# Two decoder blocks on one core: the tokens' factors as rows, by DRAM and GpSimd's queue instead of a product with ones

## The chip, the cores and the metric

The kernel runs on one core of a Trainium2 chip. The metric is the device time of one launch in microseconds. Time before: 1255.82 us, the median of three runs (1255.24 to 1256.68).

## What is computed

The reference chains two networks on 256 tokens of 1024 features. The first has two layers (a mixer of attention and a state-space part, then a mixer with a gated linear recurrence), the second has two attention layers with a shared memory. Each layer ends with a gated feed-forward part. Every part begins with an RMS norm, and that is what matters here:

```
def _rmsnorm(x, g):
    x32 = x.astype(jnp.float32)
    y = x32 * lax.rsqrt(jnp.mean(x32 * x32, axis=-1, keepdims=True) + EPS)
    return (y * g.astype(jnp.float32)).astype(x.dtype)

def swiglu(x, w_gate, w_up, w_down):
    return (jax.nn.silu(x @ w_gate) * (x @ w_up)) @ w_down
```

The factor of a token, the rsqrt, is one number for each of the 256 tokens. It commutes with the matrix product, so the kernel multiplies with the weights first and applies the factor to the product.

## The kernel before

TensorE multiplies in pairs of a rounded and a remainder part: each 512 KB tile of weights (`wr`, loaded by SyncE's queue) is rounded by ScalarE into `wh` (line 217), and VectorE subtracts to get the remainder `wl` (line 195). Four `wr` buffers, six `wh`/`wl` pairs, fifteen slots of 128 x 512 for intermediate results (`s`), six PSUM banks for products (`pm`) and two for transposes (`pt`).

The residual at the end of a part (`residual`) runs for the first half of the tokens and then for the second. It computes a mean square and asks GpSimd for a power of -1/2 (`rsqrt`, line 414, a column of 128 partitions by 1). In the first network that happens twice per half: once for the norm after the part, on which VectorE waits before it adds to `x`, and once for the factor `r` of the part that follows. In the second network only the latter exists.

With tokens in partitions, `r` is a column and can be used as a scale of one instruction. Where a product has features in partitions (`wide_t`, `linear_t`), the tokens lie along the free dimension, and the factors are wanted as a row of 256 numbers, the same in all partitions. `spread_rows` makes that: VectorE multiplies the identity by `r` for each half (`d`, line 208), TensorE multiplies a matrix of ones by `d` in plain fp32 (line 220, `pt<-s,ones`), and ScalarE copies the result to a slot (line 217, `s<-pt`). It is called five times: in each of the four `ffn` calls, after the first 512 hidden features, and once in `odd_mixer`, the recurrent mixer.

The order of the work is written by the program and by a running count of TensorE's time: `later(delay, fn)` puts a piece of work off until `pe_time` has advanced by that many microseconds, `poll` issues what is due, and `need(key)` issues what a reader must have now. `spread_rows` puts its product off by `TUNE["rows"]`, 2.0. The recording layer then sets the order within each engine.

The first reader in `ffn` is the multiply of `s` by `both` on VectorE, after a whole `wide_t` of 256 hidden features; the first in `odd_mixer` is the multiply of a bank by `rows` into `xb`, after a `linear_t` of 512 features.

Of the kernel before, what the change touches and what calls it, by code (L numbers as in the profile page):

```python
# [9 lines left out]
F32 = mybir.dt.float32  # L10
# [3 lines left out]
ALU = mybir.AluOpType  # L14
AX = mybir.AxisListType
PSUM = bass.MemoryType.PSUM

P = 128
D = 1024
# [22 lines left out]
TUNE = {  # L42
    "mla_share": 0,
    "mla_share2": 0.25,
    "lru_share": 0.35,
    "mj0": 4.5,
    "mj1": 4.5,
    "mh0": 0.0,
    "mh1": 4.5,
    "mi0": 5.0,  # L50
# [62 lines left out]
class Operand:  # L113


    def __init__(self, net, K):
        self.net, self.K = net, K
        self.quads = [None] * ((K + 3) // 4)
# [23 lines left out]
class Net:  # L142
    def __init__(self, ctx, tc, ins, plan):
        self.tc, self.nc, self.ins, self.plan = tc, tc.nc, ins, plan
        self.n = 0
        self.wall_at = 0
        self.pe_time = 0.0
        self.pending = []
        self.running = False
        self.open = []  # L150
        self.mem_r = []
        self.share = self.relief = 0.0
        e = ctx.enter_context
        self.const = e(tc.tile_pool(name="const", bufs=1))
        self.wraw = e(tc.tile_pool(name="wraw", bufs=4))
        self.wsp = e(tc.tile_pool(name="wsp", bufs=6))
        self.bigs = e(tc.tile_pool(name="bigs", bufs=11))
        self.slots = e(tc.tile_pool(name="slots", bufs=15))
        self.junk = e(tc.tile_pool(name="junk", bufs=1))
        self.small = e(tc.tile_pool(name="small", bufs=48))  # L160
        self.s5c = e(tc.tile_pool(name="s5c", bufs=1))
        self.rtab = e(tc.tile_pool(name="rtab", bufs=1))
        self.mm = e(tc.tile_pool(name="mm", bufs=6, space=PSUM))
        self.tr = e(tc.tile_pool(name="tr", bufs=2, space=PSUM))

# [198 lines left out]

    def spread_rows(self, r):

        out, d = self.slot(), self.slot()
        for h in HALVES:
            self.ts(d[:, h * P : (h + 1) * P], self.ident, r[h], ALU.mult)

        def go():
            ps = self.tbank()
            self.mmul(ps[:, 0:256], self.ones, d[:, 0:256], True, True)
            self.act(out[:, 0:256], ps[:, 0:256])

        self.later(TUNE["rows"], go, [("rows", out.name)])
        return out[:, 0:256], ("rows", out.name)

    def linear32(self, x, mat, c0, c1, sink):

# [123 lines left out]
    def ffn(self, X, r, gate, up, g_at, u_at, down, post, gains, last=False, aside=None):  # L504
        nc = self.nc
        HT = Operand(self, FF // P)
        wg = self.weights([(gate, k * P, g_at, g_at + 512) for k in range(KD)])
        wu = self.weights([(up, k * P, u_at, u_at + 512) for k in range(KD)])
        for h in HALVES:
            G, U = self.group(X, h, wg, 512), self.group(X, h, wu, 512)  # L510
            s, t = self.slot(), self.slot()
            self.act(s, G, AF.Silu, scale=r[h])
            self.mul(t, U, s)
            self.to_features(HT, h, 0, [t[:, i * P : (i + 1) * P] for i in range(4)])
        rows, key = self.spread_rows(r)
        if aside is not None:
            aside()
        mean = [self.sm() for h in HALVES]
        for h in HALVES:
            self.ts(mean[h], r[h], math.sqrt(1.0 / D), ALU.mult)  # L520
        two = lambda a: a.rearrange("p (a q) -> p a q", a=2)
        both = rows.unsqueeze(1).to_broadcast([P, 2, 256])
        for c0 in range(512, FF, 256):
            G = self.wide_t(X, gate, g_at + c0)
            self.need(key)
            s, t = self.slot(), self.slot()
            self.wide_sum(s, G)
            self.mul(two(s), two(s), both)
            self.act(s, s, AF.Silu)
            U = self.wide_t(X, up, u_at + c0)  # L530
            self.wide_sum(t, U)
            self.mul(t, t, s)
            self.heads_out(HT, c0 // P, t)
        gp = None if post is None else self.load_post(post)
        KF = FF // P
        self.flush()
        return self.rows_out(HT, down, range(KF), 5, gp, gains, last, r, mean)
# [764 lines left out]
    def odd_mixer(self, X, R):  # L1302
# [3 lines left out]
        e = self.lru_e  # L1306
# [36 lines left out]
        def conv(c):  # L1343
            self.need(("xb", c))
            for k in range(4 * c, 4 * c + 4):
                w = [self.col("conv_w", 8 * i + k) for i in range(4)]
                self.act(xc[:, k], xb[:, k], AF.Identity, scale=w[3], bias=self.col("conv_b", k))
                for lag in (1, 2, 3):
                    self.stt(xc[:, k, lag:], xb[:, k, : 256 - lag], w[3 - lag], xc[:, k, lag:], ALU.mult, ALU.add)
                self.act(v8(XH)[:, k], xc[:, k])  # L1350
                self.sub(v8(XL)[:, k], xc[:, k], v8(XH)[:, k].bitcast(F32))

        self.linear(X, "od_w_in", 0, 512, x_sink)
        self.later(TUNE["conv"], lambda: conv(0), [("xc", 0)])
        rows, key = self.spread_rows(R)
        banks = self.linear_t(X, "od_w_in", 512, 1024)
        self.need(key)
        for i, bank in enumerate(banks):
            for j in (0, 1):
                self.mul(  # L1360
# [70 lines left out]
        for i, z in enumerate(gz):  # L1431
            o = z.rearrange("p (m r j) -> p m r j", m=4, r=4)
# [405 lines left out]
```

## Time and profile before

| | |
|---|---|
| median of three runs | 1255.82 us |
| the profiled execution, its own time | 1256.24 us |
| its span on the core | 1254.5 us |
| TensorE, matmul records | busy 1237.9 us, 99% |
| VectorE | busy 879.7 us, 70% |
| ScalarE | busy 766.0 us, 61% |
| GpSimd | busy 51.3 us, 4% |
| granted TensorE clock | 0.999 of full speed |
| SyncE's load queue | 215.68 MB, 55.1% of 16 engines |

The span is the time between the core's first and last instruction; the profiled execution's own time is 1.74 us longer than its span. A busy share is taken over the whole span, and matmuls are pipelined, so that their records overlap and a busy share of 99% says that TensorE hardly ever waits, not that it works at its peak. The page's chain of waits gives 84% of the span to TensorE.

### The profile page before, as it was taken

How to read it: one execution, taken by the hardware profiler on the slowest of the kernel's cores; microseconds unless marked ns; L12 is line 12 of the kernel's file. 1: busy time of each engine (PE TensorE's matmuls, PEld its weight loads, DVE VectorE, ACT ScalarE, POOL GpSimd, SP SyncE). 2: the span in 40 equal slices, each digit the busy share in tenths (PEclk: the TensorE clock that was granted, in tenths of full speed). 3: DMA queues.
4: the chain of work that ended last, by engine and by line, in shares of the span. 5: the costliest groups of instructions: out<-in, count | busy, mean ns of one | idle time of the engine just before them, and what ended most of it. 6: DMA issues, size and time to landing. Idle time of an engine off the chain costs nothing.

```text
span 1254.5 us, 17973 instructions
## 1 busy us (share of the span) xinstructions
PE 1237.9 (99%) x6526; PEld 1036.7 (83%) x6526; DVE 879.7 (70%) x1579; ACT 766.0 (61%) x1446; POOL 51.3 (4%) x64
## 2 busy tenths in 40 slices
PE   8999999999999999999999899999999999999998
PEld 6776888888889888888887788888888888888887
DVE  7997578775588977776467855777746865677752
ACT  6767577554488766555378845555546675655531
POOL 1000000000000000000013100000000100000000
PEclk9999999999999999999999999999999999999999
DMA  8714367666555467666545224666665532666662
GB/s 269 232 52 151 118 193 230 202 189 210 154 188 178 164 193 218 191 194 204 183 150 178 85 70 149 218 185 189 213 188 152 182 118 82 205 197 187 187 198 69
DMA packets 63065, 216.83 MB, mean 173 GB/s; under 512 B 7136, under 2 KB 7520, under 8 KB 62976
## 3 DMA queue, kind: packets, MB, share of 16 engines
q1 hardware_dynamic: 62976, 215.68, 55.1%
q8 instruction: 51, 0.84, 0.3%
q14 instruction: 38, 0.31, 0.1%
HBM read 214.61 MB, written 1.05 MB: 172 GB/s over the span
## 4 chain that ended last, share of the span: by engine, by line
PE 84%; ACT 5%; DVE 5%; DMA 3%; issue 2%; POOL 1%; SPq 0%; ACTq 0%; POOLq 0%; DVEq 0%
PE pm L220 80%; PE pt L227 3%; DVE wl L195 2%; ACT j L217 1%; ACT b L217 1%; ACT wh L217 1%; DMA wr<-in_wall_dram 1%; DVE s L195 1%; ACT s L217 1%; DVE b L212 1%; POOL m L414 1%; DMA x<-in_x_dram 1%; DMA s<-in_xT_dram 1%; DMA s<-in_memT_dram 0%; ACT L217 0%
## 5 line engine op out<-in xcount | busy, mean ns | idle before, releaser
L195 DVE TENSOR_TENSOR wl<-wr,wh 128x1024 fp32r<-128x1024 f32 (+2 forms) x389 | 467.1, 1206 | 208.4 <-ACT wh L217 207.2
L220 PE MATMUL pm<-wh,b 128*128 128x512 f32 (+2 forms) x1788 | 575.4, 395 | 4.6 <-ACT wh L217 2.9
L217 ACT ACTIVATE wh<-wr 128x1024 fp32r<-128x1024 f32 (+2 forms) x381 | 397.3, 1047 | 267.2 <-PE pm L220 141.3
L220 PE MATMUL pm<-b,wh 128*128 128x512 f32 (+1 forms) x1440 | 453.2, 372 | 0.0
L220 PEld LDWEIGHTS pm<-wh,b 128*128 128x128 f32 x1788 | 334.5, 188 | 73.8 <-ACT wh L217 5.6
L220 PE MATMUL pm<-b,wl 128*128 128x256 f32 x1296 | 359.6, 278 | 0.0
L220 PE MATMUL pm<-wl,b 128*128 128x512 f32 (+2 forms) x894 | 348.8, 391 | 0.7 <-DVE wl L195 0.7
L220 PEld LDWEIGHTS pm<-b,wh 128*128 128x128 f32 x1440 | 261.1, 188 | 50.8 <-ACT b L217 0.3
L220 PEld LDWEIGHTS pm<-b,wl 128*128 128x128 f32 x1296 | 243.8, 188 | 0.3
L220 PEld LDWEIGHTS pm<-wl,b 128*128 128x128 f32 x894 | 168.6, 189 | 34.5 <-DVE wl L195 2.5
L217 ACT ACTIVATE s<-pm 128x256 f32<-128x256 f32 (+1 forms) x152 | 58.4, 386 | 66.3 <-PE pm L220 66.2
L195 DVE TENSOR_TENSOR s<-pm,s 128x256 f32<-128x256 f32 (+1 forms) x164 | 74.0, 453 | 35.5 <-ACT s L217 20.8
L414 POOL TENSOR_TENSOR m<-m,mhalf 128x1 f32<-128x1 f32 (+3 forms) x54 | 47.1, 873 | 980.2 <-DVE m L209 767.9
L195 DVE TENSOR_TENSOR s<-s,s 128x512 f32<-128x512 f32 (+3 forms) x90 | 60.5, 672 | 2.5
L217 ACT ACTIVATE b<-pt,cpk 128x128 fp32r<-128x128 f32 (+2 forms) x138 | 48.2, 390 | 8.9 <-DVE b L212 5.5
L217 ACT ACTIVATE j<-pm,m 128x128 f32<-128x128 f32 (+1 forms) x94 | 36.7, 406 | 22.4 <-PE pm L220 19.6
L227 PE MATMUL pt<-ident,s 128*128 128x128 f32 x288 | 44.1, 276 | 3.5 <-DVE s L195 2.0
L212 DVE SCALAR_TENSOR_TENSOR b<-pt,cpk,b 128x128 fp32r<-128x128 f32 x122 | 37.9, 345 | 11.4 <-ACT b L217 10.9
L227 PEld LDWEIGHTS pt<-ident,s 128*128 128x128 f32 x288 | 34.0, 142 | 14.4 <-issue 3.3
L217 ACT ACTIVATE j<-x 128x512 f32<-128x512 f32 x32 | 20.2, 631 | 27.0 <-DVE x L212 13.9
L220 PE MATMUL pm<-s,b 128*128 128x256 f32 (+1 forms) x160 | 34.6, 337 | 0.0
L220 PE MATMUL pm<-wr,s 128*128 128x512 f32 x72 | 33.4, 602 | 0.1
(162 smaller groups left out, 809.8 us busy)
## 6 DMA issues: line engine op xcount, KB each, us to landing
wr<-in_wall_dram SPq DMA_DIRECT2D x381, 512.0 KB, 3.7
wr<-in_wall_dram SPq DMA_DIRECT2D x11, 256.0 KB, 3.6
s<-in_memT_dram SPq DMA_DIRECT2D x8, 256.0 KB, 5.8
s<-in_gpost_dram SPq DMA_DIRECT2D x8, 256.0 KB, 4.8
wr<-in_wall_dram SPq DMA_DIRECT2D x4, 384.0 KB, 3.0
x<-in_x_dram SPq DMA_DIRECT2D x2, 512.0 KB, 6.9
s<-in_mem_dram SPq DMA_DIRECT2D x4, 256.0 KB, 6.0
out_dram<-x SPq DMA_DIRECT2D x4, 256.0 KB, 2.0
```

Of the source, the lines that this page charges most:

```text
L195: return self.nc.vector.tensor_tensor(out=out, in0=a, in1=b, op=op)
L212: return self.nc.vector.scalar_tensor_tensor(out=out, in0=a, scalar=s, in1=b, op0=op0, op1=op1)
L217: return self.nc.scalar.activation(out, a, func, **kw)
L220: self.nc.tensor.matmul(out, lhsT, rhs, start=start, stop=stop)
L227: self.nc.tensor.transpose(out, a, self.ident)
L414: self.nc.gpsimd.tensor_tensor(out=z, in0=w, in1=self.mhalf[:, 0:n], op=ALU.pow)
```

## The change

`spread_rows` no longer uses VectorE, TensorE or ScalarE. For each half it issues, on GpSimd's queue, a DMA that writes the column `r[h]` as 128 numbers of 4 bytes into a row in DRAM, and then one DMA that reads the row of 256 numbers back into all 128 partitions of a slot. A pool of two rows in DRAM is added. The product is no longer put off, and there is no key to ask for. One slot (`d`) fewer is taken per call.

```diff
+DRAM = bass.MemoryType.DRAM
...
+        self.rows = e(tc.tile_pool(name="rows", bufs=2, space=DRAM))
...
     def spread_rows(self, r):
 
-        out, d = self.slot(), self.slot()
+        out, row = self.slot(), self.rows.tile([1, 256], F32, name=self.name("row"), tag="row")
         for h in HALVES:
-            self.ts(d[:, h * P : (h + 1) * P], self.ident, r[h], ALU.mult)
-
-        def go():
-            ps = self.tbank()
-            self.mmul(ps[:, 0:256], self.ones, d[:, 0:256], True, True)
-            self.act(out[:, 0:256], ps[:, 0:256])
-
-        self.later(TUNE["rows"], go, [("rows", out.name)])
-        return out[:, 0:256], ("rows", out.name)
+            self.nc.gpsimd.dma_start(out=row[0, h * P : (h + 1) * P].rearrange("(p o) -> p o", o=1), in_=r[h])
+        self.nc.gpsimd.dma_start(out=out[:, 0:256], in_=row[0:1, :].to_broadcast([P, 256]))
+        return out[:, 0:256]
...
-        rows, key = self.spread_rows(r)
+        rows = self.spread_rows(r)
...
-            self.need(key)
...
-        rows, key = self.spread_rows(R)
+        rows = self.spread_rows(R)
         banks = self.linear_t(X, "od_w_in", 512, 1024)
-        self.need(key)
```

GpSimd before, at the end of the first feed-forward part: four powers, two for each half (the norm after the part, then the factor `r` of the recurrent mixer), and then the first power of the shared memory's keys.

```order
L414 TENSOR_TENSOR m_3313<-m_3307,mhalf 128x1
L414 TENSOR_TENSOR m_3325<-m_3323,mhalf 128x1
L414 TENSOR_TENSOR m_3397<-m_3391,mhalf 128x1
L414 TENSOR_TENSOR m_3409<-m_3407,mhalf 128x1
L414 TENSOR_TENSOR m_4226<-m_4217,mhalf 128x4
```

GpSimd of the change, at the same place (`rsqrt` is now line 410).

```order
L410 TENSOR_TENSOR m_3313<-m_3307,mhalf 128x1
L410 TENSOR_TENSOR m_3325<-m_3323,mhalf 128x1
L371 DMA row_3560<-m_3325 128x1
L410 TENSOR_TENSOR m_3397<-m_3391,mhalf 128x1
L410 TENSOR_TENSOR m_3409<-m_3407,mhalf 128x1
L371 DMA row_3560<-m_3409 128x1
L372 DMA s_3559<-row_3560 128x256
L410 TENSOR_TENSOR m_4224<-m_4215,mhalf 128x4
```

The three DMAs stand right behind the powers that they need and not where `spread_rows` is called: the first half's write is ahead of the second half's power for the norm after the part.

TensorE before, in the first feed-forward part, at the first `wide_t` of the gate (`pm_1889`, `pm_1890`): the transposes of the first hidden features (`pt_1924`), then the product with ones (`pt_1931`).

```order
L220 MATMUL pm_1889<-b_1612,wl_1894 128x256
L220 MATMUL pm_1890<-b_1612,wh_1893 128x512
L220 MATMUL pm_1890<-b_1612,wl_1894 128x256
L227 MATMUL pt_1924<-ident,s_1878 128x128 x4
L220 MATMUL pt_1931<-s_1882,ones 128x256
L220 MATMUL pm_1889<-b_1629,wh_1936 128x512
L220 MATMUL pm_1889<-b_1629,wl_1937 128x256
```

TensorE of the change, at the same place.

```order
L222 MATMUL pm_1892<-b_1614,wl_1897 128x256
L222 MATMUL pm_1893<-b_1614,wh_1896 128x512
L222 MATMUL pm_1893<-b_1614,wl_1897 128x256
L229 MATMUL pt_1927<-ident,s_1880 128x128 x4
L222 MATMUL pm_1892<-b_1631,wh_1936 128x512
L222 MATMUL pm_1892<-b_1631,wl_1937 128x256
```

One instruction is gone, and all else stands as it stood.

ScalarE before, a little later in the same part: the copy of the transposes, the copy of the row (`s_1881<-pt_1931`), the memory's features (`b_1903`), and the first sum of `wide_t` (`s_1958`) with the rounding of weights between.

```order
L217 ACTIVATE b_1837<-pt_1924 128x4x128
L217 ACTIVATE s_1881<-pt_1931 128x256
L217 ACTIVATE b_1903<-s_1901,cpk 128x128 x4
L217 ACTIVATE s_1958<-pm_1889 128x256
L217 ACTIVATE wh_2122<-wr_2120 128x1024
L217 ACTIVATE s_1958<-pm_1890 128x256
L217 ACTIVATE wh_2154<-wr_2152 128x1024
L217 ACTIVATE s_1956<-s_1956 128x512
```

ScalarE of the change, at the same place.

```order
L219 ACTIVATE b_1839<-pt_1927 128x4x128
L219 ACTIVATE b_1906<-s_1904,cpk 128x128 x4
L219 ACTIVATE s_1958<-pm_1892 128x256
L219 ACTIVATE s_1958<-pm_1893 128x256
L219 ACTIVATE wh_2122<-wr_2120 128x1024
L219 ACTIVATE s_1956<-s_1956 128x512
L219 ACTIVATE wh_2154<-wr_2152 128x1024
L219 ACTIVATE b_1991<-s_1989,cpk 128x128 x4
```

The copy of the row is gone, and the roundings of weights and the memory's features have changed places with copies next to them. The recurrent mixer has a few such exchanges of neighbours too, on ScalarE, VectorE and TensorE; the other three feed-forward parts only lose instructions. SyncE's queue keeps its order but for one load of the memory, which goes two loads of weights later.

## Rows read from the trace of the kernel before

**Rows 1.** The page: TensorE's busy time, and the chain by engine.

```profile
PE 1237.9 (99%) x6526; PEld 1036.7 (83%) x6526; DVE 879.7 (70%) x1579; ACT 766.0 (61%) x1446; POOL 51.3 (4%) x64
...
PE 84%; ACT 5%; DVE 5%; DMA 3%; issue 2%; POOL 1%; SPq 0%; ACTq 0%; POOLq 0%; DVEq 0%
```

**Rows 2.** Busy time by stretch, around the places of the five products.

```profile
core 0: us, PE busy (x) PEld busy (x) DVE busy (x) ACT busy (x) POOL busy (x), PEclk, DMA share, GB/s
184.00:200.00 16.00, 16.00 (x94) 14.00 (x93) 13.68 (x25) 11.10 (x22) 0.00 (x0) 1.00 0.92 302
360.00:370.00 10.00, 10.00 (x82) 9.87 (x81) 8.93 (x18) 8.49 (x15) 0.00 (x0) 1.00 0.61 204
478.00:490.00 12.00, 12.00 (x71) 10.54 (x70) 8.91 (x12) 6.42 (x11) 0.00 (x0) 1.00 0.83 273
1090.00:1100.00 10.00, 10.00 (x60) 8.78 (x59) 7.65 (x11) 5.31 (x8) 0.00 (x0) 1.00 0.86 285
```

**Rows 3.** Timeline, TensorE, recurrent mixer (start us, us, engine, line, op, tiles).

```profile
363.58 0.28 PE L220 MATMUL pm<-b,wl 128*128 128x256 f32 x1
363.70 0.59 PE L220 MATMUL pt<-s,ones 128*128 128x256 f32 x2
363.94 0.59 PE L220 MATMUL pm<-b,wh 128*128 128x256 f32 x2
364.37 0.28 PE L220 MATMUL pm<-b,wl 128*128 128x256 f32 x1
...
364.72 0.28 PE L220 MATMUL pm<-b,wl 128*128 128x256 f32 x1
```

**Rows 4.** All instructions on the tile of ones (min, median, max ns).

```profile
L220 PE MATMUL pt<-s,ones x10: 377/379/382, 188.0 to 1093.3; 128*128 128x256 f32 x10
```

**Rows 5.** Timelines of VectorE and ScalarE, recurrent mixer.

```profile
361.52 0.48 DVE L208 TENSOR_SCALAR s<-ident,m 128x128 f32<-128x128 f32 x2
...
365.11 0.36 ACT L217 ACTIVATE s<-pt 128x256 f32<-128x256 f32 x1
```

**Rows 6.** Timeline, GpSimd, at the first two of the five places.

```profile
156.39 0.56 POOL L414 TENSOR_TENSOR m<-m,mhalf 128x1 f32<-128x1 f32 x1 [3.05 <-DVE m L209]
164.66 0.55 POOL L414 TENSOR_TENSOR m<-m,mhalf 128x1 f32<-128x1 f32 x1 [7.71 <-DVE m L209]
...
344.74 0.55 POOL L414 TENSOR_TENSOR m<-m,mhalf 128x1 f32<-128x1 f32 x1 [4.08 <-DVE m L209]
348.92 0.55 POOL L414 TENSOR_TENSOR m<-m,mhalf 128x1 f32<-128x1 f32 x1 [3.64 <-DVE m L209]
353.34 0.55 POOL L414 TENSOR_TENSOR m<-m,mhalf 128x1 f32<-128x1 f32 x1 [3.87 <-DVE m L209]
```

**Rows 7.** Timeline, VectorE: the first reader of the rows, recurrent mixer.

```profile
373.86 2.07 DVE L195 TENSOR_TENSOR b<-pm,s 128x256 f32<-128x256 f32 x4
```

**Rows 8.** The page's DMA issues: the slowest and the fastest to land.

```profile
x<-in_x_dram SPq DMA_DIRECT2D x2, 512.0 KB, 6.9
...
out_dram<-x SPq DMA_DIRECT2D x4, 256.0 KB, 2.0
```

**Rows 9.** Issue of one load on SyncE; GpSimd's powers by tile (min, median, max ns).

```profile
167.85 0.33 SPq L277 DMA_DIRECT2D wr<-in_wall_dram  x1
...
L414 POOL TENSOR_TENSOR m<-m,mhalf x54: 548/702/2734, 24.4 to 1070.2; 128x1 f32<-128x1 f32 x30, 128x4 f32<-128x4 f32 x20, 128x8 f32<-128x8 f32 x2, 128x2 f32<-128x2 f32 x2
```

**Rows 10.** Timeline, VectorE: the reader of the second half's norm power.

```profile
350.59 1.40 DVE L212 SCALAR_TENSOR_TENSOR x<-s,m,x 128x512 f32<-128x512 f32 x2
```

**Rows 11.** Timeline, VectorE beside GpSimd, at two places.

```profile
27.19 1.81 POOL L999 MEMSET b<- 128x2048 f32 x1
...
27.46 1.23 DVE L195 TENSOR_TENSOR wl<-wr,wh 128x1024 fp32r<-128x1024 f32 x1
...
775.11 1.22 DVE L195 TENSOR_TENSOR wl<-wr,wh 128x1024 fp32r<-128x1024 f32 x1
...
775.34 1.41 POOL L414 TENSOR_TENSOR m<-m,mhalf 128x1 f32<-128x1 f32 x1 [9.98 <-DVE m L209]
```

## The prediction, made before the changed kernel ran

> **What bounds the kernel now.** I read the page first. TensorE's records cover 99% of the span, and the chain of waits runs through TensorE for 84% of it [rows 1]. An average over stages does not say what a change in one place is worth, so the second view is the busy time by stretch, around the places where the five products with ones stand [rows 2]: TensorE is busy for 16.00 of 16.00 us, 10.00 of 10.00, 12.00 of 12.00 and 10.00 of 10.00, at a granted clock of 1.00. (The fifth place, the third feed-forward part, has the same pattern.) VectorE and ScalarE have time left in each. So what TensorE no longer does there is time off the end, and what VectorE and ScalarE no longer do is not. The third view is TensorE's timeline, for the price of one product [rows 3]; the fourth is GpSimd's, for what stands behind the new DMAs on its queue [rows 6].
>
> **What is removed.** In the recurrent mixer the product stands between two remainder matmuls (`pm<-b,wl`) that start at 363.58 and 364.37, 0.79 us apart. The next two starts without it, 364.37 and 364.72, are 0.35 apart [rows 3]. The period of this stretch is thus 0.35 or, by the rounding of the starts, 0.36; I take 0.36, and the product costs 0.79 - 0.36 = 0.43 us. The other four stand behind a group of transposes, where no undisturbed period lies next to them, but their ten records are all alike, 377 to 382 ns [rows 4], so I take 0.43 for each: 5 x 0.43 = 2.15 us off TensorE's path. From below, the following matmul starts 0.24 us after the product (363.94 - 363.70), and from above the pair of records is 0.59 us long [rows 3]: 5 x 0.24 = 1.2 and 5 x 0.59 = 2.95.
>
> VectorE loses five pairs of multiplies of 0.48 us and ScalarE five copies of 0.36 us [rows 5]. Both count as nothing: TensorE has no idle time in these stretches that they could give back [rows 2]. If that cover were wrong, the most they could add is 5 x (0.48 + 0.36) = 4.2 us, but for that TensorE would have to be waiting for them now, and it isn't. The exchanges of neighbours on ScalarE in the first feed-forward part and in the mixer also count as nothing, for the same reason; an exchange with one rounding of weights would cost TensorE something only where it has no rounded tile in hand, and I allow half a microsecond either way for all of them.
>
> **What is added.** Ten writes of 512 B and five reads of 128 KB, all on GpSimd's queue, which issues no DMA in the trace of before. The bytes, 5 x 128 KB = 0.64 MB over the whole run, are little more than one load of 512 KB [rows 8] and count as nothing. What counts is latency, in two places.
>
> First, *the reader*. It needs the second half's write, then the read that waits for both writes. The tightest place is the recurrent mixer: the second half's power ends at 353.34 + 0.55 = 353.89 [rows 6], and VectorE reads the row at 373.86 [rows 7], 19.97 us later. What an issue on GpSimd takes no row shows. The bounds are the issue of a load on SyncE, 0.33 us, and the longest power on GpSimd, 2.73 us [rows 9]; I take the power of the same 128 x 1 column, 0.55 us, which handles the same data. Landing is between 2.0 us (the output's store, which also ends in DRAM) and 6.9 us (the slowest load) [rows 8]; I take 2.0, since these DMAs are the smallest of all. Then the row is there 2 x 0.55 + 2 x 2.0 = 5.1 us after the power, 15 us early; at the upper ends 2 x 2.73 + 2 x 6.9 = 19.3 us, still 0.7 us early. The new wait costs nothing. Nobody stands behind the read that waits on GpSimd's queue: the next power of the mixer is that of the memory's keys, and it waits for products of keys that TensorE makes only after the mixer's own.
>
> Second, *the neighbour on the queue*. The first half's write stands ahead of the second half's power for the norm after the part, on which VectorE waits before it adds to `x`. In the mixer the first half's power ends at 344.74 + 0.55 = 345.29. The next begins at 348.92, but VectorE uses it only at 350.59, behind other work [rows 6, 10], so it could begin at 350.59 - 0.55 = 350.04 and cost nothing. GpSimd has 350.04 - 345.29 = 4.75 us for the issue, more than the upper end of 2.73. In the first layer the gap is 164.66 - 156.95 = 7.7 us [rows 6], and the first network's other feed-forward part has the same pattern. In the second network no power for a norm stands behind the write. So this costs nothing either.
>
> **The sum.** The profiled execution's span of 1254.5 us becomes 1254.5 - 2.15 = 1252.35; with the 1.74 us that lie around the span, 1254.1. The median of the runs stands 0.42 us under that execution (1255.82 against 1256.24), so the forecast for the median is 1255.82 - 2.15 = 1253.7 us, 0.17% faster. About 0.2% (2.5 us) is what a measurement of this kernel can tell from no change, so the likeliest outcome lies just inside that.
>
> **The rivals.** *GpSimd's issue is slow* (slower). If writing 128 descriptors of 4 bytes keeps GpSimd for d us, the power behind it is late by d - 4.75 in the mixer and d - 7.7 in the first network's two feed-forward parts, and TensorE waits for that at the start of the next part. The gain is gone at d = 4.75 + 2.15 = 6.9 us. At d = 9.5 it is 4.75 + 2 x 1.8 = 8.35 us, less 2.15: 1262.0 us. For it speaks that no row shows such an issue; against it, that nothing on GpSimd takes more than 2.73 us now [rows 9].
>
> *GpSimd's issue holds VectorE* (slower). The two share a way to the tiles, as the trace shows: a power of one column took 1.41 us where VectorE was subtracting (775.11 to 776.33), against 0.55 alone [rows 6, 11]. If VectorE stands still for each of the ten writes, at 0.55 us each, and TensorE feels all of it, since at the joints between parts it lives on the features that VectorE makes, that is 5.5 - 2.15 = 3.4 us more: 1259.2 us (at 2.73 us each, 1280). Against it: in that row it was GpSimd that waited, and VectorE's subtraction took 1.22 us, and 1.23 us beside a fill of 1.81 us on GpSimd. The Trainium skill (SBUF — State Buffer, "SBUF: two separate sides") has a rule that speaks against the change here: the pair of ports is "an exclusive lock, not a bandwidth split", and whoever starts first, VectorE in certain operations or GpSimd, has it for the whole instruction. By that rule, the trace agrees on the half in which GpSimd waits and shows no case of the other half; the sum by the rule would be that of this rival.
>
> *The row comes late.* If both issues take 2.73 us and wait as the power did, 0.86 us more each, and both DMAs land in 6.9 us, the row is there after 21.0 us, 1.0 us late in the mixer, and in no other place. All of it on TensorE's path gives 1253.7 + 1.0 = 1254.7 us. It takes the upper end of every term at once.
>
> *Nothing comes off.* TensorE's stretches look full because matmuls overlap, and the weights' roundings could set the pace in truth; then the product's time was hidden: 1255.8 us. Against it, the starts move apart by 0.43 us at the product and are evenly spaced around it [rows 3].
>
> **How the numbers follow.** The forecast 0.68, the slow issue 0.10, VectorE held 0.08, the late row 0.08, nothing off 0.06. Within the forecast, its bounds (1.2 to 2.95 us) and the half microsecond for the exchanges put four in ten of its cases beyond 2.5 us: 0.27 for faster. The rest of it, 0.41, with 0.08 and 0.06, makes 0.55 for within 0.2%. The two slower rivals make 0.18. The range goes down to 1255.82 - 2.95 - 0.7 = 1252.2 (0.7 is half the spread of the three runs shown) and up to the price of VectorE held, 1259.2, which leaves out the slow issue, the dearer cases of VectorE held and a little below: no more than 2 in 10. The forecast's own range is 1252.2 to 1255.3.
>
> **What would show it.** Right: the remainder matmuls around the old product's place evenly spaced; TensorE without new idle time between 340 and 360 us and around the other joints; the rows landing more than 10 us ahead of their readers; GpSimd's powers at the same distance from the instructions that they wait for; VectorE's subtractions still at 1.2 us. Wrong: powers for the norm that begin later than VectorE's mean squares allow; VectorE's subtractions of 2 us beside a write; a reader that waits for a DMA; or TensorE's busy time falling by 2 us with idle time of the same size elsewhere, at the exchanged roundings first of all.

## The result: 46 us slower

The changed kernel takes 1301.59 us (median of four runs, 1298.63 to 1304.22), the kernel before 1255.53 us (four runs, 1255.06 to 1256.68): a ratio of 1.0365, 95% interval 1.0352 to 1.0379. The forecast was 1253.7 us with a range up to 1259.2. The profiled execution took 1301.69 us, its span is 1299.9 us, 45.4 more than before.

The changed kernel: from its page TensorE's busy time, the granted clock in 40 slices and the chain by line, and from its list of DMAs the new ones with their median time from issue to landing.

```profile
PE 1253.0 (96%) x6516; PEld 1045.0 (80%) x6516; DVE 878.7 (68%) x1569; ACT 765.2 (59%) x1441; POOL 60.0 (5%) x79
...
PEclk9999989999999989999999998999999999899999
...
PE pm L222 81%; DMA wr<-in_wall_dram 4%; PE pt L229 3%; ACT wh L219 1%; ACT j L219 1%; DVE wl L197 1%; DVE s L197 1%; ACT s L219 1%; POOL m L410 1%; ACT b L219 1%; DMA x<-in_x_dram 0%; DMA s<-in_xT_dram 0%; DVE b L214 0%; DMA s<-in_memT_dram 0%; DMA s<-in_rope_dram 0%
...
s<-row POOLq DMA_DIRECT2D x5, 128.0 KB, 4.7
...
row<-m POOLq DMA_DIRECT2D x10, 0.5 KB, 9.2
```

Against [rows 1] TensorE is busy 15.1 us longer (1253.0 - 1237.9) although it has ten records fewer, and of the 45.4 us the other 30.3 are new idle time. So there are two things to find: what TensorE waits for, and why its work takes longer. A write of 512 B takes 9.2 us to land, longer than any load of 512 KB in [rows 8].

What TensorE waits for, and what ScalarE waits for (engine, line, waited for: us in total, times, longest us):

```profile
PE pt L229 <- DVE x L214: 15.5, 3, 8.0
PE pt L229 <- DVE x L197: 13.4, 2, 6.7
PE pm L222 <- DVE s L197: 2.8, 2, 1.9
```

```profile
ACT wh L219 <- DMA wr<-in_wall_dram: 51.6, 25, 7.9
```

```profile
173.63 1.11 PE L229 MATMUL pt<-ident,x 128*128 128x128 f32 x4 [7.97 <-DVE x L214]
479.26 1.11 PE L229 MATMUL pt<-ident,x 128*128 128x128 f32 x4 [7.24 <-DVE x L214]
```

Four waits of 6.7 to 8.0 us make 28.6 of the 30.3 us: the two of L214 shown last (its third wait is 0.3 us) and the two of L197. They stand at the joints ahead of the four feed-forward parts, where TensorE transposes the new `x`; at the joint ahead of the recurrent mixer there is no such wait. ScalarE waited for loads of weights for 15.8 us in all before, at most 3.5 at a time; now it is 51.6 and 7.9. VectorE, which TensorE waits for at the joints, is not the cause, nor is GpSimd. The chain of waits through the first of these joints and the timeline of GpSimd show it:

```profile
158.03 12.14 DMA wr<-in_wall_dram
...
170.26 1.06 ACT wh L219
```

```profile
156.07 0.56 POOL L410 TENSOR_TENSOR m<-m,mhalf 128x1 f32<-128x1 f32 x1 [3.05 <-DVE m L211]
156.94 0.73 POOL L371 DMA_DIRECT2D row<-m  x1 [0.31 <-POOL m L410]
172.23 0.56 POOL L410 TENSOR_TENSOR m<-m,mhalf 128x1 f32<-128x1 f32 x1 [14.56 <-DVE m L211]
```

GpSimd is free again 0.73 us after it began the write at 156.94. But a load of weights that starts at 158.03 lands 12.14 us later; the median over all these loads is 3.7. ScalarE has no weights to round, TensorE runs dry, and the second half's power comes 16.16 us after the first half's (172.23 - 156.07), where it was 8.27 us in [rows 6]: 7.9 us lost at this one place. The stretches show what the DMA engines do meanwhile, first in the changed kernel, then in the kernel before:

```profile
core 0: us, PE busy (x) PEld busy (x) DVE busy (x) ACT busy (x) POOL busy (x), PEclk, DMA share, GB/s
160.00:162.00 2.00, 2.00 (x10) 1.65 (x10) 1.77 (x4) 1.81 (x4) 0.00 (x0) 1.00 1.10 35
162.00:164.00 2.00, 2.00 (x11) 1.65 (x10) 1.78 (x3) 0.34 (x2) 0.00 (x0) 1.00 1.12 39
164.00:166.00 2.00, 1.66 (x8) 1.04 (x6) 0.20 (x1) 0.00 (x0) 0.00 (x0) 1.00 0.45 29
...
172.00:174.00 2.00, 0.37 (x2) 0.37 (x3) 1.91 (x4) 0.33 (x1) 0.56 (x1) 0.50 0.26 104
174.00:176.00 2.00, 2.00 (x10) 1.82 (x9) 1.79 (x4) 1.37 (x5) 0.42 (x1) 0.50 0.00 0
```

```profile
160.00:162.00 2.00, 2.00 (x11) 1.65 (x10) 1.88 (x4) 1.60 (x4) 0.00 (x0) 1.00 0.65 211
162.00:164.00 2.00, 2.00 (x10) 1.68 (x9) 1.78 (x4) 1.85 (x4) 0.00 (x0) 1.00 0.86 305
```

The engines count as full (shares of 1.10 and 1.12) and move 35 and 39 GB/s, where they moved 211 and 305. It is not the new write that fills them. The DMA queues from 158 to 168 us (packets, MB, share of 16 engines), SyncE's loads and then GpSimd's queue in the changed kernel, and SyncE's loads before:

```profile
q1 hardware_dynamic: 174, 0.63, 96.4%
q0 software_dynamic: 32, 0.00, 0.2%
```

```profile
q1 hardware_dynamic: 667, 2.42, 74.6%
```

The packets of the write take 0.2% of the engines' time. Those of the loads take nearly all of it for a quarter of the bytes: 0.89 us a packet (0.964 x 160 us / 174) where it was 0.18 (0.746 x 160 / 667). So while the write is under way the loads' own packets are slow.

In the idle stretch the granted clock falls to 0.50, the level of 1.2 GHz, and stays there until past 176 us, so TensorE is also slower when it starts again. Five stretches at 0.50, four of them at the four waits, hold 20.4 us of TensorE's busy time, against 3.4 us before. A matmul of 512 columns takes 0.78 us there and 0.40 at 1.00, so an estimate of what the clock adds is half of the difference, 8.5 of the 15.1 us.

The rest is something else. The groups of TensorE's instructions with their shapes (count | busy us, mean ns | idle before), the changed kernel:

```profile
L222 PE MATMUL pm<-b,wh 128*128 128x512 f32 x1152 | 407.6, 399 | 0.0
L222 PE MATMUL pm<-b,wl 128*128 128x256 f32 x1296 | 364.1, 281 | 0.0
```

and the kernel before:

```profile
L220 PE MATMUL pm<-b,wh 128*128 128x512 f32 x1152 | 400.6, 394 | 0.0
L220 PE MATMUL pm<-b,wl 128*128 128x256 f32 x1296 | 359.6, 278 | 0.0
```

These are the pairs of the feed-forward parts' `wide_t` stretches, 288 pairs in each of the four (the second group has 144 more, in the mixer), with nothing waiting ahead of them. They are the same instructions, and they became slower. The timeline of the first stretch tells where. Before, around the product and at the end:

```profile
184.79 0.39 PE L220 MATMUL pm<-b,wh 128*128 128x512 f32 x1
...
187.25 0.40 PE L220 MATMUL pm<-b,wh 128*128 128x512 f32 x1
187.49 0.28 PE L220 MATMUL pm<-b,wl 128*128 128x256 f32 x1
187.61 0.60 PE L227 MATMUL pt<-ident,s 128*128 128x128 f32 x4
188.04 0.60 PE L220 MATMUL pt<-s,ones 128*128 128x256 f32 x2
188.29 0.58 PE L220 MATMUL pm<-b,wh 128*128 128x512 f32 x1
188.71 0.27 PE L220 MATMUL pm<-b,wl 128*128 128x256 f32 x1
188.82 0.40 PE L220 MATMUL pm<-b,wh 128*128 128x512 f32 x1
...
285.19 0.40 PE L220 MATMUL pm<-b,wh 128*128 128x512 f32 x1
```

After the change:

```profile
196.37 0.60 PE L229 MATMUL pt<-ident,s 128*128 128x128 f32 x4
196.73 0.48 PE L222 MATMUL pm<-b,wh 128*128 128x512 f32 x1
197.04 0.28 PE L222 MATMUL pm<-b,wl 128*128 128x256 f32 x1
197.16 0.40 PE L222 MATMUL pm<-b,wh 128*128 128x512 f32 x1
...
295.38 0.40 PE L222 MATMUL pm<-b,wh 128*128 128x512 f32 x1
```

Ahead of the product the kernel before steps by (187.25 - 184.79) / 7 = 351 ns from pair to pair; the first of the seven steps is 340 ns, the other six have a mean of 353.3. Behind it, from the second pair (188.82) to the last (285.19), 278 steps take 96.37 us: 346.7 ns a step. In the changed kernel the same 278 steps take 98.22 us: 353.3 ns. The other three stretches have the same two paces (353.2 to 353.3 ns after, 346.8 before, over all steps of a stretch but the two at the transposes). So TensorE has two steady paces for the same pairs, and it seems to be the product that puts it into the quicker one; the experiments test that. Without it the slower one would stay to the end of the stretch: 280 pairs x 6.6 ns x 4 parts = 7.4 us.

### The profile page after: what moved, and what is told of

Read it like the earlier page. It is cut to its first block, busy times and chain, and to the rows that moved or that the text cites. A ratio compares the mean times of both kernels' runs of the same rounds, so it can differ in the third digit from the quotient of the medians.

```text
span 1299.9 us, 17966 instructions
## 1 busy us (share of the span) xinstructions
PE 1253.0 (96%) x6516; PEld 1045.0 (80%) x6516; DVE 878.7 (68%) x1569; ACT 765.2 (59%) x1441; POOL 60.0 (5%) x79
## 4 chain that ended last, share of the span: by engine, by line
PE 84%; DMA 5%; ACT 4%; DVE 4%; issue 1%; POOL 1%; SPq 0%; ACTq 0%; DVEq 0%; POOLq 0%
PE pm L222 81%; DMA wr<-in_wall_dram 4%; PE pt L229 3%; ACT wh L219 1%; ACT j L219 1%; DVE wl L197 1%; DVE s L197 1%; ACT s L219 1%; POOL m L410 1%; ACT b L219 1%; DMA x<-in_x_dram 0%; DMA s<-in_xT_dram 0%; DVE b L214 0%; DMA s<-in_memT_dram 0%; DMA s<-in_rope_dram 0%
## 5 line engine op out<-in xcount | busy, mean ns | idle before, releaser
L197 DVE TENSOR_TENSOR wl<-wr,wh 128x1024 fp32r<-128x1024 f32 (+2 forms) x389 | 467.4, 1206 | 216.9 <-ACT wh L219 214.9
L222 PE MATMUL pm<-b,wh 128*128 128x512 f32 (+1 forms) x1440 | 460.4, 376 | 2.7 <-DVE s L197 1.9
L222 PE MATMUL pm<-b,wl 128*128 128x256 f32 x1296 | 364.1, 281 | 0.0
L197 DVE TENSOR_TENSOR s<-pm,s 128x256 f32<-128x256 f32 (+1 forms) x164 | 73.9, 453 | 36.9 <-ACT s L219 21.5
L197 DVE TENSOR_TENSOR s<-s,s 128x512 f32<-128x512 f32 (+3 forms) x90 | 60.6, 673 | 2.5
L214 DVE SCALAR_TENSOR_TENSOR b<-pt,cpk,b 128x128 fp32r<-128x128 f32 x122 | 38.1, 346 | 31.2 <-ACT b L219 30.7
L229 PE MATMUL pt<-ident,x 128*128 128x128 f32 x112 | 20.4, 319 | 29.0 <-DVE x L214 15.5
L229 PEld LDWEIGHTS pt<-ident,x 128*128 128x128 f32 x112 | 15.4, 163 | 34.7 <-DVE x L214 18.1
```

The lines of the kernel that those rows point to most:

```text
L197: return self.nc.vector.tensor_tensor(out=out, in0=a, in1=b, op=op)
L214: return self.nc.vector.scalar_tensor_tensor(out=out, in0=a, scalar=s, in1=b, op0=op0, op1=op1)
L222: self.nc.tensor.matmul(out, lhsT, rhs, start=start, stop=stop)
L229: self.nc.tensor.transpose(out, a, self.ident)
```

## The experiments

Two questions: what makes ten writes of 512 B so dear, and does the lost product really cost TensorE its pace. The expectations weigh three theories for the first: pieces (a write in pieces of 4 B keeps the DMA engines from the loads), queue (any DMA that GpSimd issues holds the loads up) and read-back (the read of 128 KB does). Runs with a single execution can be off by 2 to 4 us (the kernel before ran from 1254.4 to 1258.1 us in seven runs beside the first four, and from 1253.7 to 1259.1 in 25 beside the next). The diffs show the lines that matter; `...` stands for what is left out.

**The writes alone.** The kernel before, product kept, with the ten column writes put in and never read.

```diff
+        row = self.rows.tile([1, 256], F32, ...)
+        for h in HALVES:
+            self.nc.gpsimd.dma_start(out=row[0, h*P:(h+1)*P].rearrange("(p o) -> p o", o=1), in_=r[h])
         out, d = self.slot(), self.slot()
...
```

> The kernel before, with its product, and at each of the five places also the two writes of the column into DRAM, which nobody reads; no read-back. Pieces expects the whole loss on top of the kernel before, with the product still paid: 1298 to 1308 us; queue expects two thirds, 1284 to 1290 us; read-back expects 1255 to 1258 us.

Measured: 1293.15 us, against 1255.13 for the kernel before. The ten writes alone cost 38.0 of the 46.1 us. That is 5 us under the range of the theory of pieces and 3 above that of the queue; the next runs decide between them. The waits of TensorE are much the same as in the changed kernel:

```profile
PE pt L229 <- DVE x L197: 13.0, 2, 6.6
PE pt L229 <- DVE x L214: 12.1, 3, 6.5
```

**Another queue.** The changed kernel with its ten writes issued by ScalarE.

```diff
-            self.nc.gpsimd.dma_start(out=row[0, ...
+            self.nc.scalar.dma_start(out=row[0, ...
```

> Three theories of where the 46 us come from. Pieces: a write of 128 pieces of 4 bytes into DRAM occupies the 16 DMA engines for some 8 us, whoever issues it, and loads of weights behind it land late. Queue: a DMA that GpSimd issues holds the loads up, whatever its pieces are. Read-back: the broadcast read of 128 KB holds them up. Here ScalarE issues the ten writes and GpSimd only the five reads. Pieces expects 1290 to 1310 us and writes that still land after 8 us or more; queue expects a third of the loss, 1265 to 1272 us, and writes that land in some 2 us; read-back expects 1295 to 1305 us.

Measured: 1283.45 us, and 8.9 us to landing. The figure fits none of the three theories: it lies below what pieces and read-back expect and above what the queue expects. But the landing doesn't change with the queue, so it is not GpSimd's way of issuing. Why it is 18 us less: on ScalarE the first half's write stands behind other work, and in the first part it goes out at 162.64 (156.94 in the changed kernel). The first joint is then passed without a wait, and loads that start later are late instead. A load that starts at 174.01 takes 9.45 us. Whether this moving accounts for all of the 18 us was not tried.

**Reads alone.** The kernel before with five reads of 128 KB from a fixed row in DRAM that nothing uses.

```diff
+        spare = self.s5c.tile([P, 256], F32, name="spare", tag="spare")
+        self.nc.gpsimd.dma_start(out=spare, in_=self.kept[0:1, :].to_broadcast([P, 256]))
         out, d = self.slot(), self.slot()
...
```

> The kernel before, with its product, and at each of the five places also a broadcast read of a fixed DRAM row by GpSimd whose result nobody reads. Pieces expects 1255 to 1259 us; queue expects a third of the loss, 1268 to 1274 us; read-back expects the whole loss, 1298 us or more.

Measured: 1260.99 us, but the run doesn't answer the question. The reads depend on nothing, so all five went out between 5.7 and 29.7 us, where the first loads run, and the first feed-forward part's wide stretch already begins 3 us later than before. The reads in their own places are in the runs below.

**Longer pieces.** In place of 128 pieces of 4 B, VectorE turns the two columns (a 32 x 32 block transpose), and one write of 8 pieces of 128 B goes out. The read-back is kept.

```diff
-            self.nc.gpsimd.dma_start(out=row[0, ...], in_=r[h])
+            self.nc.vector.tensor_copy(self.turn[:, 32 * h : 32 * h + 1], r[h])
+        self.nc.vector.transpose(self.turned, self.turn)
+        self.nc.gpsimd.dma_start(out=row.rearrange("o (h b j) -> (o b) h j", h=2, b=4),
+                                 in_=self.turned[::32, :].rearrange("b (h j) -> b h j", h=2))
...
```

> The changed kernel, but VectorE first turns the column into four pieces of 32 numbers for each half (a transpose in blocks of 32), and one write of 8 pieces of 128 bytes takes the place of the two writes of 128 pieces of 4 bytes. Reads as in the change. Pieces expects the loss gone and the product's 2.15 us saved: 1252.5 to 1255 us, with no load of weights landing late; queue expects two thirds of the loss, 1280 to 1290 us; read-back expects 1295 to 1305 us.

Measured: 1261.61 us (1260.23 to 1262.15), ratio 1.0050, interval 1.0033 to 1.0067. The DMAs of this run:

```profile
s<-row POOLq DMA_DIRECT2D x5, 128.0 KB, 3.4
...
row<-turned POOLq DMA_DIRECT2D x5, 1.0 KB, 2.3
```

40 of the 46 us are gone, and no wait of TensorE is longer than 1.8 us. But 6 us are left that the expectation didn't have. The wide pairs of this run step by 353.3 ns in all four parts, which gave the theory of the two paces. The next three runs test it.

**No rows at all.** Product and DMAs both left out; the readers multiply by a fixed tile of ones, so the result lacks the tokens' factors.

```diff
-        out, row = self.slot(), self.rows.tile(...)
-        ...
-        return out[:, 0:256]
+        return self.flat
...
```

> The kernel before with the rows left out of the computation: no product, no DMA, the readers multiply by a fixed tile of ones. Rhythm theory (in the 288 wide pairs of each feed-forward layer TensorE steps by 353.3 ns a pair up to the product and by 346.7 ns behind it, so the product sets the quicker step; without it the slower one stays, 280 pairs x 6.6 ns x 4 layers = 7.4 us): about 1255.5 - 2.2 + 7.4 = 1260.7 us, wide pairs at 353.3 ns, no wait that is not in the kernel before. Rival (the 6 us that the long-piece kernel still lost belong to its transfers): removing the product alone gives 2.2 us back, about 1253.4 us, pairs at 346.7 ns.

Measured: 1260.32 us (ratio 1.0038, interval 1.0027 to 1.0049), with the two groups of wide matmuls at 407.6 and 364.1 us as in the changed kernel, and at 353.3 ns a pair in each part. Taking five products away, with nothing put in, costs 4.8 us.

**A product that nothing reads**, 256 columns, beside the long pieces.

```diff
...
+        self.later(TUNE["rows"], lambda: self.mmul(self.tbank()[:, 0:256], self.ones, self.flat, True, True))
```

> The long-piece kernel (1261.6 us) with a product of ones by a fixed tile, 128 by 256, put on TensorE where the old product stood; nothing reads it. Rhythm theory: the four wide stretches go back to 346.7 ns a pair, 1261.6 - 7.4 + 4 x 0.43 = 1255.9 us (1255 to 1257). Rival (the transfers cost it): 1261.6 + 1.7 = 1263.3 us.

Measured: 1256.50 us (ratio 1.0003, interval 0.9992 to 1.0014), and the pace is back:

```profile
L222 PE MATMUL pm<-b,wh 128*128 128x512 f32 x1152 | 400.6, 394 | 0.0
L222 PE MATMUL pm<-b,wl 128*128 128x256 f32 x1296 | 359.6, 278 | 0.0
```

**A shorter one**, 128 columns.

```diff
-... self.mmul(self.tbank()[:, 0:256], self.ones, self.flat, True, True)
+... self.mmul(self.tbank()[:, 0:P], self.ones, self.ident, True, True)
```

> As the one before, with a product of 128 columns in place of 256 (0.21 us in place of 0.43 by columns). Rhythm theory, if any other instruction between two wide stretches resets the step: about 1255.0 us, pairs at 346.7 ns. If the reset hangs on the shape of the instruction in between: pairs stay at 353.3 ns and about 1262.4 us. Rival (transfers): 1262.4 us, whatever the pairs do.

Measured: 1255.00 us (ratio 0.9990, interval 0.9979 to 1.0001), 346.7 ns a pair in all four parts. Adding a matmul of no use to the long-piece kernel makes it 6.6 us faster. The transfers of that kernel, the read-back of 128 KB among them, cost nothing that these runs can tell.

The second question: **what about the pieces is dear**, their number, their size or their place? Four kernels, each the one before with ten unused writes of 128 pieces by GpSimd, product kept, so that all are read against 1293 us (4 B side by side in DRAM).

512 B each (for this and the 64 B, VectorE first copies the factor into a tile, so that the write waits for it):

```diff
+        row = self.rows.tile([P, P], F32, ...)
+        for h in HALVES:
+            self.nc.vector.tensor_copy(self.wide[:, h : h + 1], r[h])
+            self.nc.gpsimd.dma_start(out=row, in_=self.wide)
...
```

> The kernel before with ten unused writes of 128 pieces of 512 bytes each (64 KB) from GpSimd, product kept, in place of ten unused writes of 128 pieces of 4 bytes (which gave 1293 us). If the number of pieces costs: again 1285 to 1300 us and a landing of 8 us or more. If the smallness of the pieces costs: 1255 to 1260 us, landing of 2 to 4 us.

4 B each, in rows 1024 B apart:

```diff
+        row = self.rows.tile([P, 2 * P], F32, ...)
+        for h in HALVES:
+            self.nc.gpsimd.dma_start(out=row[:, h * P : h * P + 1], in_=r[h])
```

> The kernel before with ten unused writes from GpSimd of 128 pieces of 4 bytes, as in the run that gave 1293 us, but each piece into a row of its own in DRAM, 1024 bytes apart. If a piece costs because it is small: 1285 to 1300 us again, landing 7 to 10 us. If the pieces get in each other's way because they fall on the same 512 bytes: 1255 to 1260 us, landing 2 to 4 us.

4 B each, side by side in SBUF:

```diff
+        for h in HALVES:
+            self.nc.gpsimd.dma_start(out=self.inrow[0:1, h * P : (h + 1) * P], in_=r[h])
...
```

> The same ten writes of 128 pieces of 4 bytes, side by side, into one partition of SBUF in place of DRAM. If small pieces cost wherever they go: 1285 to 1300 us, landing 7 to 10 us. If DRAM is part of the price: 1255 to 1265 us, landing under 5 us.

64 B each, side by side in DRAM:

```diff
+        row = self.rows.tile([P, 16], F32, ...)
+        for h in HALVES:
+            self.nc.vector.tensor_copy(self.wide[:, h : h + 1], r[h])
+            self.nc.gpsimd.dma_start(out=row, in_=self.wide)
...
```

> The kernel before with ten unused writes of 128 pieces of 64 bytes (8 KB, side by side in DRAM), from GpSimd, behind the copy of the factor into the tile as in the run with pieces of 512 bytes (1257 us). If the price falls with the size of the piece: between 1257 and 1293 us, landing 3 to 8 us. If only pieces of a few bytes cost: 1256 to 1258 us, landing under 3 us.

Measured, one execution each: 1256.99, 1255.03, 1254.50 and 1257.68 us. The write's row in the DMA issues, in the order 4 B side by side, then 512 B, 4 B apart, 4 B into SBUF, 64 B:

```profile
row<-m POOLq DMA_DIRECT2D x10, 0.5 KB, 8.5
```

```profile
row<-wide POOLq DMA_DIRECT2D x10, 64.0 KB, 2.8
```

```profile
row<-m POOLq DMA_DIRECT2D x10, 0.5 KB, 3.1
```

```profile
inrow<-m POOLq DMA_DIRECT2D x10, 0.5 KB, 3.0
```

```profile
row<-wide POOLq DMA_DIRECT2D x10, 8.0 KB, 2.9
```

In all of them there are 128 pieces. Only where they are of 4 B, in DRAM, and next to each other does a write take 8.5 us and the kernel lose 38. A piece of 4 B alone is not dear (3.1 us in rows apart), nor is their number, nor DRAM. The Trainium skill (DMA: Bandwidth & Descriptors, "Why small descriptors are slow (HBM only)") has small pieces slow because each carries a fixed overhead, and exempts transfers from SBUF to SBUF. The trace agrees for SBUF (3.0 us); by that rule the pieces 1024 B apart would have been as slow as those side by side, and they were not (3.1 against 8.5 us), so here the place decides. What DRAM does with neighbouring pieces, and at which distance between 4 and 1024 B, or at which size between 4 and 64 B, it ends, no run shows.

**Both causes out.** The changed kernel with the factors gathered into a row of SBUF, one write of 1 KB to DRAM, the same read-back, and the idle product of 128 columns.

```diff
-            self.nc.gpsimd.dma_start(out=row[0, ...], in_=r[h])
+            self.nc.gpsimd.dma_start(out=self.inrow[0:1, h * P : (h + 1) * P], in_=r[h])
+        self.nc.gpsimd.dma_start(out=row, in_=self.inrow)
         self.nc.gpsimd.dma_start(out=out[:, 0:256], in_=row[0:1, :].to_broadcast([P, 256]))
+        self.later(TUNE["rows"], lambda: self.mmul(self.tbank()[:, 0:P], self.ones, self.ident, True, True))
...
```

> The changed kernel with both causes taken out: the two halves' factors are written as 4-byte pieces into a row of SBUF, one write of 1 KB takes the row to DRAM, the read-back follows as before, and a product of 128 columns that nothing reads stands on TensorE where the old one stood. Theory (pieces side by side in DRAM cost 38 us, the lost quicker step 7.4 us, nothing else costs): 1254.5 to 1255.5 us, no wait of TensorE over 2 us, wide pairs at 346.7 ns. If transfers issued by GpSimd or the read-back of 128 KB also cost: above 1258 us.

Measured: 1254.11 us (12 runs, 1252.62 to 1258.03; ratio 0.9992, interval 0.9981 to 1.0002). That is 0.4 us under the range expected, and all 46 us are back. The wide pairs are at 346.7 ns in all four parts. The costliest of TensorE's waits, and the DMAs (no single wait is longer than 1.5 us):

```profile
PE pt L229 <- DVE s L197: 2.0, 3, 1.1
```

```profile
s<-row POOLq DMA_DIRECT2D x5, 128.0 KB, 4.9
...
inrow<-m POOLq DMA_DIRECT2D x10, 0.5 KB, 2.9
...
row<-inrow POOLq DMA_DIRECT2D x5, 1.0 KB, 1.6
```

It can't be told from the kernel before. Of the 0.43 us that leaving out a product gives back, the idle one of half the columns takes 0.22 us again, by the starts around it.

## Why the prediction was wrong, point by point

The price of 46.1 us is made of 38.0 (the writes, in the run with them alone) and 4.8 (the products gone, in the run without rows). The 3.3 us between their sum and the whole stay open: single executions scatter by as much, and the waits for `x` at the joints are also longer in the changed kernel (28.9 against 25.1 us by the lines above).

- **The step that failed first: "The bytes ... are little more than one load of 512 KB and count as nothing. What counts is latency".** The DMA was costed by its bytes and its landing alone, as if it could not touch other transfers. What counted is what it does to them: while a write of 512 B was under way, the loads of weights beside it took up to 10 to 12 us (median of all 3.7), and TensorE waited 6.7 to 8.0 us at four joints. The write's own packets took 0.2% of the engines' time there; why the loads' packets are slow beside it stays open. The rows had a hint that the loads could not spare the time: the DMA engines' share is 0.83 to 0.92 in three of the four stretches of [rows 2], and 0.65 and 0.86 in the two rows of the kernel before shown above, at the joint itself. A load that is 8 us late there was not hidden.
- **Landing**, taken as 2.0 us with 6.9 as the upper end, was 9.2 (up to 11.6). The reason given, that these are the smallest transfers of all, was wrong for pieces of 4 B side by side, and nearer the mark for the same bytes elsewhere (1.6 to 3.1 us). No row of the kernel before had such a transfer; both ends came from rows of large pieces, so the range didn't hold the case. The upper end was no bound even for those: 6.9 us is a median, the slowest that the page lists, and in the same trace the one load of `b<-in_s_bc_dram`, 512 KB, took 7.6 us.
- **The second step that failed: "5 x 0.43 = 2.15 us off TensorE's path".** The product's own price was about right: 1260.32 - 1255.52 = 4.8 is 7.4 - 2.15 to within half a microsecond. What was missing is that its neighbours' pace depends on it. The period was read in the mixer [rows 3], where the pace is 360 ns on both sides of the product; in the other four places the prediction noted that no undisturbed period lay next to the product, and carried the mixer's over. The steps ahead of it and behind it in those four, 353.3 (but for the first) and 346.7 ns, were there to be read.
- **What held.** The reader waited for nothing: no engine but GpSimd itself waits for a row. GpSimd's issue took 0.54 to 0.73 us (0.55 taken), so the rival of a slow issue didn't come about, though its sign was right. VectorE was not held: its subtractions have a mean of 1206 ns in both kernels. VectorE's and ScalarE's removed work gave nothing back that the runs can tell, and the row was not late, though in the mixer it landed at 382.58 and was read at 387.24, 4.7 us ahead and not 15.
- **Rivals.** All four looked at GpSimd, VectorE, the reader and TensorE; none at the queue that the change doesn't touch, SyncE's loads. Of the signs of being wrong that it named none came: the power at 172.23 is later than before, but not later than VectorE's mean squares allow, for GpSimd was waiting for VectorE there (14.56 us). What failed is a sign of being right, no new idle time of TensorE around the other joints. (For VectorE held at 2.73 us for each write the prediction has 1280 us; its terms give 1281.0.)

## What to carry to other kernels

Cost a DMA by what it does to the transfers that other queues have under way, not by its bytes or its landing alone, and look in the trace at how long those take beside it; above all, don't write a column of 4-byte values as neighbours into DRAM while loads are due. Gather it in SBUF or turn it first. (Spread pieces were quick to write; reading them back was not tried.) And where TensorE has no idle time, compare the step of the matmuls on both sides of an instruction before counting its removal as a gain: here a product that nothing read set the pace behind it.

## What was not expected of the hardware

- A write of 128 pieces of 4 B side by side in DRAM landed in 8.5 to 9.2 us from GpSimd's queue and 8.9 from ScalarE's (medians). Beside the first of them, from 160 to 166 us, the 16 DMA engines moved 29 to 39 GB/s at shares of 0.45 to 1.12. Its own packets took 0.2% of the engines' time from 158 to 168 us; the loads' packets took 0.89 us each on the mean, 0.18 before. The same 128 pieces took 3.1 us in rows 1024 B apart and 3.0 into SBUF; pieces of 64 B side by side took 2.9.
- TensorE runs the same pairs of matmuls (512 and 256 columns) at 346.7 or 353.3 ns, and keeps either pace over 280 pairs. A product of ones, of 128 or 256 columns, between a group of transposes and the stretch gave the quicker pace every time (in all four parts of each of the ten kernels that had it). With the transposes alone it was the slower one in all four parts of the changed kernel, the long-piece kernel and the one without rows, and in three parts of the ScalarE kernel. In its first part the ScalarE kernel ran at 346.7 ns without a product, behind a stretch of 3.4 us at a granted clock of 0.50. Why there are two paces, and what of the instruction in between decides, stays open.
